# Eight gate sums moved from GpSimd to VectorE, and one accumulator bank taken from another pool

## The chip, the cores and the metric

The kernel runs on one core of a Trainium2 chip. The time is that of one execution on the device, in microseconds. A core has five engines that matter here: TensorE (PE, with its weight loads as PEld), VectorE (DVE), ScalarE (ACT), GpSimd (POOL) and SyncE (SP), which issues most of the DMAs. GpSimd also issues some DMAs, those that add to what they find in memory. Each engine takes its instructions strictly in order.

## What is computed

One decoder layer on 512 tokens of width 1024, all in float32. Three branches are computed from the normalised input u, each an attention and a projection, and each is weighted by a gate:

```python
g = jax.nn.sigmoid(gl.reshape(B, S, N_BRANCH, D))
merged = (g[:, :, 0] * jnp.einsum('bse,ed->bsd', y_swa, w_branch_swa[l])
          + g[:, :, 1] * jnp.einsum('bse,ed->bsd', y_sb, w_branch_sb[l])
          + g[:, :, 2] * jnp.einsum('bse,ed->bsd', y_mem, w_branch_mem[l]))
mix = jnp.einsum('bsd,de->bse', merged, w_out[l])
h = h + rms_norm(mix, ln_mix_post[l])
```

The branches are attention over a band of 128 tokens (swa), stick-breaking attention (sb) and cross-attention to 256 memory vectors (mem, four heads of width 128). A gated feed-forward network of width 2816 follows.

## The kernel before

**Products.** Everything is kept transposed, with 128 channels on the partitions and the 512 tokens along the row. A float32 product is made of three: each factor is split into a high part and a low part (`split`, lines 135 and 136: a cast on ScalarE, a subtraction on VectorE), and `mm3` issues high by high, low by high and high by low (lines 169, 171 and 172). So a factor has to be loaded, cast and subtracted before TensorE can use it.

**Order of the work.** The weights of the projections, gates and branches form one list of units (`dn`). Each unit has a load (ahead by four units), a split (ahead by three) and a generator that issues its products. The attention code runs these products in between: `dn.run(us)` issues units for so many estimated microseconds while softmax work goes on elsewhere. The branches come in the order stick-breaking, banded, memory. A scheduler then places the instructions of each engine by its own estimates and by priority, so the order on an engine isn't the order of the code; code under `tc.high_priority()` goes ahead.

**Joining the branches** (`branch`, from line 578). For each of eight channel blocks c, twelve products give a branch product in an accumulator bank `br`. VectorE multiplies it by the gate (line 592, into the gate's tile `g`). For the stick-breaking branch that tile becomes the accumulator. For the banded branch (`order == 1`) GpSimd adds the tile to the accumulator (line 598). For the memory branch VectorE adds it (line 600), and the result is split for the output projection. The banded branch's eight products are run while the four memory heads go through their softmax (`mem_pair`): scores `ms`, a maximum (line 957) and its negation (line 960), exponentials on ScalarE, a reciprocal (line 965), scalings `mw` on VectorE (line 968), transposes `mpt` on TensorE (line 974), their splits `mpts` (lines 135 and 136), value products `ym` and their splits `y2`.

**The memory gates** are computed as a product of 2x2 blocks with seven instead of eight block products (`quarter`, `add_quarters`), named p1, p2, p5, p6, p3, p7, p4 and taken in this order, twice (n = 0 and 1). Three accumulator banks hold them: x for p1, p6, p7 and p4 on top of each other, w for p2, y for p5 and p3. Each block product is 24 products of 256 columns. In the trace these banks are qx, qw and qy. Behind p1, p5 and p6 ScalarE copies the bank (line 415, `qkp`); behind p2, p3 and p7 VectorE joins the bank and an earlier copy (line 409; for p2 the result is `qj`). The factor of p5 is a sum that a DMA of GpSimd makes (line 377); VectorE then adds p1's weights to it for p6 and p2's for p3 (line 393).

**Accumulator banks.** TensorE has eight banks. Two make up the pool `psd` (`dps`), which takes the units' products: projections, branch products and, before the change, all three banks of the gates. Six make up `psa` (`aps`), which takes the attention's tiles and later the output projection and the feed-forward network. A new tile takes a bank that its last user has given up.

Of the kernel before, what the change touches and what calls it, by code (L numbers as in the profile page):

```python
# [14 lines left out]
ALU = mybir.AluOpType  # L15
# [11 lines left out]
SWA, SB, MEM = 0, 1, 2  # L27
# [76 lines left out]
def tile_kernel(ctx, tc, a):  # L104
    nc = tc.nc
# [12 lines left out]
    def ck(name, dt=F32):  # L118
        return ckp.tile([P, 512], dt, tag="ck", name=name)
# [4 lines left out]
    def dps(name):  # L124
        return psd.tile([P, 512], F32, tag="d", name=name)
# [6 lines left out]
    def split(raw, hi, lo, sign=1.0):  # L132

        if sign == 1.0:
            ins = nc.scalar.copy(hi, raw)  # L135
            lows = nc.vector.tensor_tensor(lo, raw, hi.bitcast(F32), op=ALU.subtract)  # L136
        else:
            ins = nc.scalar.mul(hi, raw, sign)
            lows = nc.vector.scalar_tensor_tensor(lo, raw, sign, hi.bitcast(F32), op0=ALU.mult, op1=ALU.subtract)
        if "behind" in st:  # L140
            after(ins, st["behind"][0])
            after(lows, st["behind"][1])
        return ins
# [23 lines left out]
    def mm3(out, l, r, start, stop, right_last=False):  # L167
        (lh, ll), (rh, rl) = l, r
        one = nc.tensor.matmul(out, lh, rh, start=start, stop=False, skip_group_check=True)  # L169
        two, three = ((ll, rh), (lh, rl)) if right_last else ((lh, rl), (ll, rh))  # L170
        nc.tensor.matmul(out, *two, start=False, stop=False, skip_group_check=True)  # L171
        return one, nc.tensor.matmul(out, *three, start=False, stop=stop, skip_group_check=True)  # L172
# [4 lines left out]
    def cols(hl, o, n):  # L177
        return hl[0][:, o : o + n], hl[1][:, o : o + n]
# [175 lines left out]
    TILE = dict(p1="x", p6="x", p7="x", p4="x", p5="y", p3="y", p2="w")  # L354
    SEVEN = ("p1", "p2", "p5", "p6", "p3", "p7", "p4")
    qw, qb_, qk = {}, {}, {}

    def right_of(p, k):
        if p in ("p1", "p2"):
            return tuple(x[:, :256] for x in u[k if p == "p1" else 4 + k])  # L360
        if p in ("p5", "p3"):
            return tuple(x[:, 256:] for x in u[k if p == "p5" else 4 + k])
        return cols(right[p][k // 2], (k % 2) * 256, 256)
# [33 lines left out]
    def q_end(b, n, p, ps):  # L397
        def done(i, f, src, sign=1.0):
            if b in st.get("sigmoid", ()):
                gate_out(b, n, i, f, src, sign)  # L400
                return
            if sign != 1.0:
                t = ck(f"qr{b}{n}")
                nc.scalar.mul(t[:, :], src[:, :], sign)
                src = t
            st.setdefault(("raw", b), []).append((n, i, f, src))

        def join(t, x, y, op, i, f):
            nc.vector.tensor_tensor(t[:, :], x[:, :], y[:, :], op=op)
            done(i, f, t)  # L410

        with tc.high_priority():
            if p in ("p1", "p5", "p6"):
                qk[p] = ck(f"qk{p}{b}{n}")
                nc.scalar.copy(qk[p][:, :], ps[:, :])
            elif p == "p3":
                t = qk.pop("p6")
                join(t, t, ps, ALU.subtract, 1, 0)
            elif p == "p7":
                t = qk.pop("p5")  # L420
                join(t, t, ps, ALU.subtract, 1, 1)
            elif p == "p2":
                t = ck(f"qj{b}{n}")
                join(t, ps, qk.pop("p1"), ALU.add, 0, 0)
            else:
                done(0, 1, ps, -1.0)

    def quarter(b, n, p):
        def gen(hi, lo):
            if p in ("p1", "p5", "p2"):  # L430
                qb_[TILE[p]] = dps(f"q{TILE[p]}{b}{n}")
            ps = qb_[TILE[p]]
            for j in range(2):
                for k in range(4):
                    first = p in ("p1", "p5", "p2") and j == 0 and k == 0
                    mm3(
                        ps[:, j * 256 : (j + 1) * 256], cols((hi, lo), (j * 4 + k) * P, P), right_of(p, k), first, k == 3
                    )
                    yield 0.36
            q_end(b, n, p, ps)  # L440

        return gen
# [139 lines left out]
    def branch(b, c2, order):  # L582
        def gen(hi, lo):
            for i in range(2):
                c = 2 * c2 + i
                g = st[(f"g{b}", c)] if (f"g{b}", c) in st else quart[(b, c)]
                ps = dps(f"br{b}{c}")
                for k in range(4):
                    mm3(ps[:, :], cols((hi, lo), (i * 4 + k) * P, P), y[(b, k)], k == 0, k == 3)
                    yield 0.65  # L590
                with tc.high_priority():
                    nc.vector.tensor_tensor(g[:, :], ps[:, :], g[:, :], op=ALU.mult)
                if order == 0:
                    st[("acc", c)] = g
                    continue
                acc = st[("acc", c)]
                if order == 1:
                    nc.gpsimd.tensor_tensor(acc[:, :], acc[:, :], g[:, :], op=ALU.add)
                    continue
                nc.vector.tensor_tensor(acc[:, :], acc[:, :], g[:, :], op=ALU.add)  # L600
                h, l = ck(f"mgh{c}", F32R), ck(f"mgl{c}", F32R)
                split(acc[:, :], h[:, :], l[:, :])
                merged[c] = (h, l)

        return gen
# [4 lines left out]
    for h in range(2):  # L610
        for q in range(3):
            n = 3 if q < 2 else 2
# [677 lines left out]
    bank = {}  # L1290
# [316 lines left out]
```

## Time and profile before

| | us |
|---|---|
| median of three runs | 812.18 |
| lowest and highest of them | 811.28, 813.80 |
| the profiled execution, its own time | 813.66 |
| its span, first to last instruction | 811.9 |
| TensorE busy | 798.1 |
| VectorE busy | 619.0 |
| ScalarE busy | 476.7 |
| GpSimd busy | 91.6 |
| mean granted clock of TensorE | 0.995 |

The profile is one execution. A row of its timeline has the start, the duration, the engine, the line in the code, the operation with what it writes and reads, how many such instructions in a row it stands for, and in brackets how long the engine was idle before it and for whom it waited. In a row of a source line stand the shortest, median and longest duration in nanoseconds. Matmuls are pipelined: one that is listed with 0.39 us lets the next start after about 0.23, so the distance from start to start tells the cost, not the listed duration. The granted clock is a share of full speed.

### The profile page before, as it was taken

What the parts mean: (1) busy time and instruction counts of PE and PEld (TensorE: products, weight loads), DVE (VectorE), ACT (ScalarE), POOL (GpSimd) and SP (SyncE); (2) the same over time, 40 slices, a digit from 0 to 9 for tenths busy, and PEclk for the clock granted to TensorE, in tenths of its full rate; (3) what the DMA queues carried; (4) which work ended last, traced back from release to release, by engine and by line L of the source; (5) the groups of instructions that cost most, each with busy time, mean ns of one, the idle gap of its engine ahead of it and who ended that gap; (6) DMA issues with size and microseconds to landing.
All of it is one profiled execution on the core that took longest, in us unless ns stands there. A gap on an engine that the chain in (4) does not pass through costs nothing.

```text
span 811.9 us, 12928 instructions
## 1 busy us (share of the span) xinstructions
PE 798.1 (98%) x4939; PEld 709.7 (87%) x4939; DVE 619.0 (76%) x975; ACT 476.7 (59%) x861; POOL 91.6 (11%) x109
## 2 busy tenths in 40 slices
PE   9999999999999999899999999999999999999996
PEld 6899788778788889689988899999999999988885
DVE  6898678545478887696694869977676777898797
ACT  7466686665766555555572566655555555666673
POOL 1102110000000000331004100100000000205200
PEclk9999999999999999999999999999999999999998
DMA  9343445212241406505568935987777662759902
GB/s 306 128 147 104 141 157 165 70 52 71 61 104 62 120 3 183 128 27 130 156 226 293 252 60 136 265 210 202 189 178 190 179 171 86 177 132 222 209 2 103
DMA packets 41726, 117.68 MB, mean 145 GB/s; under 512 B 4768, under 2 KB 6320, under 8 KB 41664
## 3 DMA queue, kind: packets, MB, share of 16 engines
q1 hardware_dynamic: 31584, 87.77, 33.8%
q0 software_dynamic: 9648, 28.82, 18.9%
q8 instruction: 38, 0.62, 0.3%
q10 hardware_dynamic: 432, 0.27, 0.1%
q14 instruction: 24, 0.20, 0.1%
HBM read 113.18 MB, written 3.67 MB: 144 GB/s over the span
## 4 chain that ended last, share of the span: by engine, by line
PE 50%; DVE 2%; issue 1%; ACT 1%; DVEq 0%
PE gx L172 5%; PE gx L169 5%; PE gx L171 5%; PE x L172 2%; PE x L171 2%; PE x L169 2%; PE gy L169 2%; PE gy L172 2%; PE gy L171 2%; PE mx L172 2%; PE mx L169 2%; PE mx L171 2%; PE y L172 1%; PE y L171 1%; PE y L169 1%; PE gw L172 1%
## 5 line engine op out<-in xcount | busy, mean ns | idle before, releaser
L135 ACT CAST hi<-gw 128x1024 fp32r<-128x1024 f32 x77 | 79.8, 1047 | 81.4 <-DVE gw L1192 39.8
L136 DVE TENSOR_TENSOR lo<-gw,hi 128x1024 fp32r<-128x1024 f32 x77 | 93.6, 1223 | 34.0 <-ACT hi L135 33.9
L135 ACT CAST hi<-raw 128x1024 fp32r<-128x1024 f32 (+2 forms) x52 | 53.1, 1032 | 49.3 <-PE qb L171 11.3
L136 DVE TENSOR_TENSOR lo<-raw,hi 128x1024 fp32r<-128x1024 f32 (+2 forms) x52 | 63.1, 1217 | 18.7 <-ACT hi L135 18.5
L1174 POOL DMA_DIRECT2D gw<-in_w_gu x27 | 23.3, 895 | 190.4 <-DMA gw<-in_w_gu 117.7
L135 ACT CAST hi<-r 128x1024 fp32r<-128x1024 f32 (+1 forms) x24 | 23.6, 981 | 19.9 <-PE y L172 5.3
L171 PE MATMUL x<-lo,lh 128*128 128x512 f32 x88 | 34.3, 390 | 0.0
L169 PE MATMUL x<-hi,lh 128*128 128x512 f32 x88 | 34.3, 389 | 0.0
L172 PE MATMUL x<-hi,ll 128*128 128x512 f32 x88 | 34.1, 389 | 0.0
L136 DVE TENSOR_TENSOR lo<-qw,hi 128x1024 fp32r<-128x1024 f32 x18 | 22.8, 1264 | 11.2 <-ACT hi L135 11.2
L136 DVE TENSOR_TENSOR lo<-r,hi 128x1024 fp32r<-128x1024 f32 (+1 forms) x24 | 27.2, 1132 | 3.9 <-ACT hi L135 3.7
L135 ACT CAST hi<-qw 128x1024 fp32r<-128x1024 f32 x18 | 18.9, 1050 | 16.2 <-issue 6.0
L188 ACT ACTIVATE e<-e 128x384 f32<-128x384 f32 (+1 forms) x48 | 26.9, 561 | 1.5
L834 DVE SCALAR_TENSOR_TENSOR e<-z,e 128x384 f32<-128x384 f32 (+1 forms) x24 | 14.3, 598 | 17.6 <-ACT e L188 17.6
L135 ACT CAST hi<-bp 128x512 fp32r<-128x512 f32 x33 | 19.3, 620 | 13.5 <-PE y L172 4.8
L136 DVE TENSOR_TENSOR lo<-bp,hi 128x512 fp32r<-128x512 f32 x33 | 22.2, 708 | 5.7 <-ACT hi L135 5.5
L172 PE MATMUL gx<-N2h,lo 128*128 128x256 f32 x88 | 25.0, 285 | 0.3 <-DVE lo L136 0.3
L169 PE MATMUL gx<-B11h,hi 128*128 128x256 f32 x88 | 25.1, 285 | 0.2 <-ACT B11h L1103 0.2
L169 PE MATMUL mx<-woh,mgh 128*128 128x512 f32 x64 | 25.0, 391 | 0.0
L172 PE MATMUL gw<-B21h,lo 128*128 128x256 f32 x88 | 25.0, 284 | 0.0
L171 PE MATMUL gx<-B11l,hi 128*128 128x256 f32 x88 | 25.0, 284 | 0.0
L172 PE MATMUL mx<-woh,mgl 128*128 128x512 f32 x64 | 24.9, 390 | 0.0
(920 smaller groups left out, 2986.4 us busy)
## 6 DMA issues: line engine op xcount, KB each, us to landing
gw<-in_w_gu SPq DMA_DIRECT2D x57, 512.0 KB, 5.1
gw<-in_w_gu POOLq DMA_DIRECT2D x27, 512.0 KB, 6.9
raw<-in_w_p SPq DMA_DIRECT2D x26, 512.0 KB, 4.1
qw<-in_w_p SPq DMA_DIRECT2D x15, 512.0 KB, 4.0
raw<-in_w_br SPq DMA_DIRECT2D x12, 512.0 KB, 3.9
bp<-in_w_dn SPq DMA_DIRECT2D x22, 256.0 KB, 8.7
r<-in_w_dn POOLq DMA_DIRECT2D x10, 512.0 KB, 8.1
raw<-in_w_out SPq DMA_DIRECT2D x8, 512.0 KB, 4.5
```

Source lines behind the costliest of these rows:

```text
L135: ins = nc.scalar.copy(hi, raw)
L136: lows = nc.vector.tensor_tensor(lo, raw, hi.bitcast(F32), op=ALU.subtract)
L169: one = nc.tensor.matmul(out, lh, rh, start=start, stop=False, skip_group_check=True)
L171: nc.tensor.matmul(out, *two, start=False, stop=False, skip_group_check=True)
L172: return one, nc.tensor.matmul(out, *three, start=False, stop=stop, skip_group_check=True)
L188: ins = nc.scalar.activation(*args, **kw)
L834: nc.vector.scalar_tensor_tensor(x, z[i][:, :n], 0.0, x, op0=ALU.max, op1=ALU.add)
L1174: nc.gpsimd.dma_start(gw[(n, key)][:, :], g_src(n, i, j), accum_op=ALU.add)
```

## The change

Two edits. The sums that add the banded branch to the accumulator are issued on VectorE instead of GpSimd. In the memory gates the bank y, which p5 opens and p3 uses after it, comes from the pool of six (`aps`) instead of the pool of two (`dps`); the banded branch's gates keep theirs.

```diff
     def quarter(b, n, p):
         def gen(hi, lo):
             if p in ("p1", "p5", "p2"):
-                qb_[TILE[p]] = dps(f"q{TILE[p]}{b}{n}")
+                bank = aps if b == MEM and p == "p5" else dps
+                qb_[TILE[p]] = bank(f"q{TILE[p]}{b}{n}")
...
                 if order == 1:
-                    nc.gpsimd.tensor_tensor(acc[:, :], acc[:, :], g[:, :], op=ALU.add)
+                    nc.vector.tensor_tensor(acc[:, :], acc[:, :], g[:, :], op=ALU.add)
                     continue
```

The scheduler places other instructions differently in consequence. From line 432 on, the changed kernel's lines have numbers higher by one.

On VectorE, at the start of the banded branch, before: the gate products (line 592, on the branch products br), the first head's reciprocal and scalings, and the second head's.

```order
L592 TENSOR_TENSOR g_2970<-br_3403,g_2970 128x512
L957 TENSOR_REDUCE mnm_3366<-ms_3334 128x2
L957 TENSOR_REDUCE mnm_3366<-ms_3335 128x2
L960 TENSOR_SCALAR mnm_3366<-mnm_3366 128x4
L965 RECIPROCAL mden_3351<-mden_3351 128x4
L968 TENSOR_SCALAR mw_3348<-mw_3348,mden_3351 128x256 x2
L592 TENSOR_TENSOR g_3307<-br_3424,g_3307 128x512
L968 TENSOR_SCALAR mw_3349<-mw_3349,mden_3351 128x256 x2
L136 TENSOR_TENSOR lo_3421<-qw_3382,hi_3420 128x1024
```

The same place on VectorE in the changed kernel; line 599 is the moved sum:

```order
L599 TENSOR_TENSOR g_1761<-g_1761,g_2891 128x512
L593 TENSOR_TENSOR g_2970<-br_3403,g_2970 128x512
L958 TENSOR_REDUCE mnm_3366<-ms_3334 128x2
L958 TENSOR_REDUCE mnm_3366<-ms_3335 128x2
L599 TENSOR_TENSOR g_1810<-g_1810,g_2970 128x512
L966 RECIPROCAL mden_3351<-mden_3351 128x4
L961 TENSOR_SCALAR mnm_3366<-mnm_3366 128x4
L593 TENSOR_TENSOR g_3307<-br_3424,g_3307 128x512
L969 TENSOR_SCALAR mw_3348<-mw_3348,mden_3351 128x256 x2
L969 TENSOR_SCALAR mw_3349<-mw_3349,mden_3351 128x256 x2
L136 TENSOR_TENSOR lo_3421<-qw_3382,hi_3420 128x1024
```

Two sums stand among the others, and all four scalings of the first head now come behind the gate product g_3307.

On TensorE, at the first head's transposes, before: the transposes of the first scaled half, three products of the fourth channel block, then the transposes of the second half.

```order
L974 MATMUL mpt_3434<-c_ident,mw_3348 128x128
L974 MATMUL mpt_3435<-c_ident,mw_3348 128x128
L171 MATMUL br_3475<-y00l,hi_3240 128x512
L172 MATMUL br_3475<-y00h,lo_3241 128x512
L169 MATMUL br_3475<-y01h,hi_3240 128x512
L974 MATMUL mpt_3434<-c_ident,mw_3349 128x128
L974 MATMUL mpt_3435<-c_ident,mw_3349 128x128
```

The same place on TensorE in the changed kernel, up to the first transposes:

```order
L171 MATMUL br_3475<-y00l,hi_3240 128x512
L172 MATMUL br_3475<-y00h,lo_3241 128x512
L169 MATMUL br_3475<-y01h,hi_3240 128x512
L171 MATMUL br_3475<-y01l,hi_3240 128x512
L172 MATMUL br_3475<-y01h,lo_3241 128x512
L975 MATMUL mpt_3434<-c_ident,mw_3348 128x128
L975 MATMUL mpt_3435<-c_ident,mw_3348 128x128
```

Six products of br_3475 now stand in front of the transposes, where one stood before, and the transposes of both halves follow in one piece.

On TensorE, in the memory gates with n = 0, before: p2 has ended, nine products of p6 (qx) have begun, and p5 (qy) comes behind them; these are the last four of the nine and the first of p5.

```order
L172 MATMUL qx_3775<-p6rh_2919,lo_3772 128x256
L169 MATMUL qx_3775<-p6rh_2990,hi_3771 128x256
L171 MATMUL qx_3775<-p6rl_2991,hi_3771 128x256
L172 MATMUL qx_3775<-p6rh_2990,lo_3772 128x256
L169 MATMUL qy_3845<-n0h,hi_3607 128x256
L171 MATMUL qy_3845<-n0l,hi_3607 128x256
L172 MATMUL qy_3845<-n0h,lo_3608 128x256
```

The same place on TensorE in the changed kernel, from the last products of p2 (qw) on:

```order
L169 MATMUL qw_3807<-n7h,hi_3573 128x256
L171 MATMUL qw_3807<-n7l,hi_3573 128x256
L172 MATMUL qw_3807<-n7h,lo_3574 128x256
L169 MATMUL qy_3845<-n0h,hi_3607 128x256
L171 MATMUL qy_3845<-n0l,hi_3607 128x256
L172 MATMUL qy_3845<-n0h,lo_3608 128x256
L169 MATMUL qy_3845<-n1h,hi_3607 128x256
```

p5 follows p2 directly, and p6's 24 products stand in one piece behind p5. With n = 1 the same happens, where fourteen products of p6 stood in front of p5.

## The prediction

> **What bounds the kernel now.** I read the page first, then TensorE's own list of waits, then windows around the place where those waits lie, then the timeline of that place. The page says that TensorE works nearly all the time:
>
> ```profile
> span 811.9 us, 12928 instructions
> PE 798.1 (98%) x4939; PEld 709.7 (87%) x4939; DVE 619.0 (76%) x975; ACT 476.7 (59%) x861; POOL 91.6 (11%) x109
> ```
>
> So time can only come out of TensorE's 13.8 us of idleness, or out of stretches in which it works slowly. Its waits on other engines are few (total, times, longest, in us):
>
> ```profile
> PE mpt L974 <- DVE mw L968: 3.0, 1, 3.0
> PE qy L169 <- DVE qj L409: 0.8, 1, 0.8
> PE qy L169 <- ACT qkp L415: 0.4, 1, 0.4
> ```
>
> All three lie in the part of the program that the change touches: the first in the banded branch, where the memory attention's weights are transposed (mpt), the other two in the memory gates' products (qy). The windows, with busy time and count of TensorE, weight loads, VectorE, ScalarE and GpSimd, then granted clock, DMA share and GB/s:
>
> ```profile
> 334.87:350.42 15.55, 12.36 (x65) 10.04 (x64) 14.14 (x21) 6.78 (x16) 5.00 (x4) 0.89 0.21 35
> 350.42:366.00 15.58, 15.58 (x78) 12.89 (x77) 14.14 (x26) 9.22 (x25) 5.04 (x3) 1.00 0.12 34
> 339.60:343.00 3.40, 3.21 (x10) 2.73 (x11) 3.37 (x10) 1.07 (x2) 0.00 (x0) 0.50 0.40 72
> 343.00:344.00 1.00, 1.00 (x11) 0.91 (x9) 0.59 (x1) 0.00 (x0) 0.00 (x0) 1.00 0.00 0
> 430.00:460.00 30.00, 30.00 (x134) 24.86 (x133) 17.99 (x36) 12.11 (x30) 12.58 (x11) 1.00 0.98 294
> ```
>
> The first half of the banded stage lasts as long as the second with fewer products in it, and the granted clock in it is 0.50 from 339.6 to 343 and 1.00 again behind that. The timeline tells why:
>
> ```profile
> 335.87 1.19 POOL L377 DMA_DIRECT2D qw<-in_w_p  x1 [4.15 <-ACT hi L135]
> 336.06 3.93 DVE L968 TENSOR_SCALAR mw<-mw,mden 128x256 f32<-128x256 f32 x2
> 336.34 0.40 PE L169 MATMUL br<-y01h,hi 128*128 128x512 f32 x1
> 336.65 2.92 POOL L598 TENSOR_TENSOR g<-g,g 128x512 f32<-128x512 f32 x2
> 339.79 1.12 PE L974 MATMUL mpt<-c_ident,mw 128*128 128x128 f32 x4 [3.05 <-DVE mw L968]
> ```
>
> Two small scalings on VectorE take 3.93 us and end when GpSimd's DMA issue and its two sums (L598) have ended; TensorE's next transposes wait for them. That this is GpSimd's doing shows in the groups by shape (busy, then mean ns):
>
> ```profile
> L968 DVE TENSOR_SCALAR mw<-mw,mden 128x256 f32<-128x256 f32 x16 | 9.1, 621 | 0.1
> L919 DVE TENSOR_SCALAR w<-w,den 128x256 f32<-128x256 f32 x32 | 9.2, 349 | 0.2
> L393 DVE TENSOR_TENSOR qw<-qw,qw 128x1024 f32<-128x1024 f32 x6 | 9.3, 1545 | 0.1
> L1192 DVE TENSOR_TENSOR gw<-gw,gw 128x1024 f32<-128x1024 f32 x20 | 24.4, 1219 | 0.0
> L600 DVE TENSOR_TENSOR g<-g,g 128x512 f32<-128x512 f32 x8 | 5.5, 685 | 0.0
> L598 POOL TENSOR_TENSOR g<-g,g x8: 1282/1502/2457, 330.4 to 367.6; 128x512 f32<-128x512 f32 x8
> ```
>
> The scaling that runs among the sums has a mean of 621 ns, the same shape elsewhere 349. The weight addition L393 has 1545 against 1219 for its twin. The sums themselves reach 2457 ns. The Trainium skill's page "SBUF — State Buffer", section "Who interferes with whom", says that VectorE and GpSimd share one pair of memory ports as an exclusive lock, for scalings and for sums with two SBUF inputs alike. The trace agrees: the scaling was held until 339.7.
>
> **The change, part 1: the eight sums go to VectorE.** What the stage loses today follows from what its instructions cost where nothing holds them:
>
> ```profile
> 350.06 0.28 PE L169 MATMUL ms<-mks1h,qms3h 128*128 128x256 f32 x1
> 350.18 0.28 PE L171 MATMUL ms<-mks1l,qms3h 128*128 128x256 f32 x1
> 350.42 0.40 PE L169 MATMUL br<-y00h,hi 128*128 128x512 f32 x1
> 353.17 0.39 PE L169 MATMUL br<-y00h,hi 128*128 128x512 f32 x1
> 357.93 1.91 PE L974 MATMUL mpt<-c_ident,mw 128*128 128x128 f32 x16
> 359.60 0.48 PE L169 MATMUL br<-y03h,hi 128*128 128x512 f32 x1
> ```
>
> A score product (ms) follows the one before it after 0.12 us. Twelve 512-column products lie between 350.42 and 353.17, so each is 0.229. Sixteen transposes take 359.60 - 357.93 = 1.67. By the code, the first half (334.87 to 350.42) holds 12 branch and 12 value products, 24 score products and 16 transposes: 24 x 0.229 + 24 x 0.12 + 1.67 = 10.05 us. It takes 15.55, so 5.5 are lost: 3.05 of idleness, 1.6 by the clock (half of the 3.21 us in which TensorE worked at 0.50), the rest in small waits. The second half holds 60 such products and 16 transposes, 15.41 us, and takes 15.58.
>
> What the stage will lose after the change I replay along VectorE's new order, with these rows:
>
> ```profile
> 332.35 0.69 DVE L592 TENSOR_TENSOR g<-br,g 128x512 f32<-128x512 f32 x1 [2.00 <-PE br L172]
> 332.96 1.28 DVE L957 TENSOR_REDUCE mnm<-ms 128x2 f32<-128x512 f32 x2
> 334.64 0.39 PE L172 MATMUL br<-y03h,lo 128*128 128x512 f32 x1
> 341.25 1.14 DVE L968 TENSOR_SCALAR mw<-mw,mden 128x256 f32<-128x256 f32 x4
> ```
>
> Instructions of that size start 0.61 apart (332.35 to 332.96), and a scaling follows another after (1.14 - 0.35) / 3 = 0.26. The two reductions let go at 334.24. The new sum of g_1810 takes 0.6, to 334.84, and reciprocal and negation 0.4, to 335.24. The product on br_3424, ready at 335.03, comes next, to 335.84. Then come the four scalings at 335.84, 336.11, 336.37 and 336.64. TensorE meanwhile has six products of br_3475 in front of the transposes, now moved ahead of them: 334.87 + 6 x 0.229 = 336.24. The first scaling is done at 336.19, the last at 336.99, so the eight transposes end at 337.2, with a wait of 0.15. The next head's transposes, and the first value products that need mpts00l, come out 0.25 late in the same way. In the second half the transposes of head 3 stand behind the product g_3313, which waits for its branch product; there I find 0.25 more. This gives 0.65 us of new waits, none near 3 us, so no clock loss.
>
> What the replay leaves open is GpSimd's DMA issue at 335.87, which stays and falls on the first scaling. The row before shows the scaling held from 336.06, 0.59 us before the sums began, though it needs 0.35; so the DMA issue may hold it too. Its bounds are 0 (the scaling is first, at 335.84) and 1.2 (a whole issue). The nearest row is this same one; which of the two comes first is open within 0.03 us, so I take 0.5. The stage then loses 0.65 + 0.5 = 1.15 instead of 5.5 + 0.17 = 5.67: a gain of **4.5 us**.
>
> VectorE's load covers this. It is busy 28.28 of 31.13 us in the stage; the eight sums add 8 x 0.685 = 5.5, and the stretching that ends gives back 16 x (621 - 349) + 6 x (1545 - 1219) ns = 6.3. Behind the sums on VectorE's queue stand the scalings that the transposes need; that delay is in the replay. GpSimd keeps its weight DMAs, and the sums no longer stand between them; the last waited for a split on VectorE and not for a sum, so nothing is won there:
>
> ```profile
> 375.11 1.20 POOL L377 DMA_DIRECT2D qw<-in_w_p  x1 [5.41 <-DVE lo L136]
> 358.15 1.22 DVE L136 TENSOR_TENSOR lo<-qw,hi 128x1024 fp32r<-128x1024 f32 x1
> ```
>
> The Trainium skill's page "TensorE: Matmul & The Clock Gate", section "What's actually happening", says the clock halves after about 3.4 us of idleness, in a free-running window. Here 3.05 us were enough in the profiled run; by the page it depends on where the window falls, so a timed run may lack the 1.6 us. By that the gain would be 6.2 - 1.6 = 4.6 in such a run.
>
> **Part 2: the bank of p5.** With two banks, qx holds one and qw the other, so qy had to wait until the join qj had emptied qw:
>
> ```profile
> 372.72 0.28 PE L172 MATMUL qx<-p6rh,lo 128*128 128x256 f32 x1
> 373.79 0.39 PE L169 MATMUL qy<-n0h,hi 128*128 128x256 f32 x1 [0.79 <-DVE qj L409]
> 394.61 0.28 PE L171 MATMUL qx<-p6rl,hi 128*128 128x256 f32 x1
> 395.00 0.39 PE L169 MATMUL qy<-n0h,hi 128*128 128x256 f32 x1
> 399.06 0.28 PE L172 MATMUL qx<-p6rh,lo 128*128 128x256 f32 x1
> 399.69 0.39 PE L169 MATMUL qy<-n4h,hi 128*128 128x256 f32 x1 [0.35 <-ACT qkp L415]
> ```
>
> Against a step of 0.12 these three cost 0.95 + 0.27 + 0.51 = 1.73. With a bank of the six, p5 follows p2 at once; its factor was split at 358.15 (the second row above), 15 us before its use. p6 then runs in one piece behind it, so its factor is due later, and p5's copy has 24 products (2.9 us) of cover before p3 needs the bank. I take all of it: **1.7 us**, bounds 0 and 1.7. The six banks' other users, the memory heads, have been emptied by then.
>
> **Sum.** 4.5 + 1.7 = 6.2 us. From 405 on TensorE runs without a hole until the mix (30.00 of 30.00 in the last window above), so what is won early should arrive at the end. The profiled execution took 813.66 (span 811.9 and 1.76 around it), so 813.66 - 6.2 = **807.5 us**. The median of the three runs shown is 812.18, 1.5 lower, about the size of the clock loss; 812.18 - 4.6 gives 807.6, so I leave the forecast there.
>
> **Rivals.** About 0.3%, 2.4 us, is what a measurement of this kernel can tell from no change.
> - *Small waits at every transpose.* GpSimd's DMA issue holds the scalings for a full 1.2 us, each of the four groups of transposes waits 0.6, and 1.0 of the bank's 1.7 is won: 5.67 - 3.6 + 1.0 = 3.1, so 810.6 from the profiled run and 809.1 from the median; I put it at 809.7. For it: VectorE stays 90% busy in order. Against it: the replay's margins.
> - *The gain is absorbed later, or timed runs lack the hole.* From 430 to 460 the DMA share is 0.98; if those loads don't start earlier, the feed-forward's first weights come late by what was won: 812. Against it: TensorE has no hole there, and buffers that the moving work empties release the loads.
> - *VectorE becomes the bound, slower.* If the long rows are VectorE's own and stay, it has 28.28 + 5.5 = 33.8 us of work in a stage of 31.13. That adds 2.7, and two more holes of 3 us cost 1.6 of clock each; less 1.7 for the bank, 813.66 + 4.2 = 817.9. It decides where a scaling stays over 1 us with no sum beside it. Against it: 32 scalings of that shape at 349 ns.
> - *The change doesn't do what it says* would mean that p5 still waits; then 1.7 is missing and the time is 809.2, inside the first rival.
>
> **How the numbers follow.** Forecast 0.62; first rival with the last 0.16; absorbed 0.15; slower 0.07. The low end is the full 7.2 us (no new wait but 0.2) off the median, 805.0; the high end, 810.8, takes in the first rival and the upper edge of the forecast, and leaves the other two out. Faster by over 2.4 us is the forecast and most of the first rival, 0.76; within it 0.17; slower 0.07.
>
> **What would show it.** Right: L968 back near 350 ns each, L393 near 1220, no TensorE wait on mw above 1 us, the granted clock at 1.00 through the stage, no idle row before qy, and the stage shorter by 4 to 5 us. The DMA issue would show as one L968 of up to 1.5 us. Wrong: a TensorE wait of 2 us or more on mw or mpts, a clock window of 0.50, or a new wait on a weight load behind 430.

## The result, and the profile after

The changed kernel takes 806.76 us (median of 4 runs, 806.60 to 806.88), the kernel before 812.73 beside it (4 runs, 811.28 to 813.80): a ratio of 0.9928, with a 95% interval of 0.991 to 0.9945. Run again later (e11 below) it took 806.74 against 813.76, a ratio of 0.9919 (0.9905 to 0.9932). The profiled execution took 806.6 us, 1.8 of it around the span. Two of the 41 runs of the kernel before that were timed beside the experiments took 1595.41 and 4496.57 us, and no number here counts them.

The page of the changed kernel, span and busy time by engine:

```profile
span 804.8 us, 12915 instructions
PE 795.6 (99%) x4939; PEld 708.2 (88%) x4939; DVE 616.2 (77%) x983; ACT 477.0 (59%) x861; POOL 78.9 (10%) x101
```

TensorE has as many instructions as before and 2.5 us less busy time; 4.6 us of its idleness have gone as well. VectorE has taken on eight sums and is 2.8 us less busy than before. TensorE's list of waits begins so (total, times, longest):

```profile
PE warm L175 <- DVE idle L683: 1.4, 1, 1.4
PE gx L172 <- DVE lo L136: 0.3, 1, 0.3
PE kb L169 <- ACT uh L245: 0.2, 1, 0.2
```

All three lie outside the part that was changed, and the list of the kernel before had them too, with 1.3, 0.3 and 0.4 us; the three rows that the prediction shows were not all of it. The waits at mpt and qy are gone. The scalings are now L969, their transposes L975, the sums L599. The stretch of the stage in which the long wait and the slow clock lay, in four windows, and then longer ones, with the columns as in the prediction:

```profile
335.00:338.00 3.00, 3.00 (x18) 2.45 (x17) 2.90 (x8) 3.00 (x11) 1.19 (x1) 1.00 0.00 1
338.00:339.60 1.60, 1.60 (x9) 1.17 (x9) 1.60 (x5) 1.46 (x3) 0.00 (x0) 1.00 1.04 125
339.60:341.50 1.90, 1.90 (x13) 1.61 (x12) 1.90 (x6) 0.76 (x3) 0.00 (x0) 1.00 0.93 169
341.50:343.00 1.50, 1.50 (x10) 1.32 (x9) 1.50 (x4) 1.06 (x3) 0.00 (x0) 1.00 0.05 12
...
334.97:360.95 25.98, 25.98 (x142) 21.71 (x140) 24.86 (x52) 16.80 (x41) 1.19 (x1) 1.00 0.20 41
360.95:398.44 37.49, 37.49 (x313) 37.46 (x312) 24.47 (x24) 20.18 (x31) 1.20 (x1) 1.00 0.54 155
422.90:452.90 30.00, 30.00 (x134) 24.85 (x133) 18.40 (x36) 12.11 (x30) 12.23 (x11) 1.00 0.97 294
398.44:804.80 406.36, 399.04 (x2656) 368.61 (x2654) 321.87 (x481) 227.44 (x396) 52.34 (x56) 1.00 0.67 174
```

TensorE is busy in all of the first four, and their granted clock is 1.00. The fifth row is the whole banded stage, 25.98 us where it was 31.13. The sixth is the memory gates' products. For those, and for all that follows, the windows of the kernel before, cut at the same two instructions:

```profile
366.00:405.54 39.54, 38.29 (x313) 37.65 (x312) 24.85 (x23) 20.56 (x32) 3.33 (x2) 1.00 0.54 146
405.54:811.90 406.36, 399.02 (x2656) 368.65 (x2654) 321.69 (x481) 227.40 (x396) 52.69 (x56) 0.99 0.67 174
```

So the gates are 2.05 us shorter, the stage 5.15, and the remainder takes 406.36 us both times: what was won arrives at the end whole. The seventh row above is the mix, the window that the prediction shows at 430 to 460, seven microseconds earlier and without a hole.

VectorE's groups by shape (busy, then mean ns), after:

```profile
L920 DVE TENSOR_SCALAR w<-w,den 128x256 f32<-128x256 f32 x32 | 9.2, 348 | 0.2
L393 DVE TENSOR_TENSOR qw<-qw,qw 128x1024 f32<-128x1024 f32 x6 | 7.3, 1222 | 0.1
L599 DVE TENSOR_TENSOR g<-g,g 128x512 f32<-128x512 f32 x8 | 5.4, 678 | 0.0
L969 DVE TENSOR_SCALAR mw<-mw,mden 128x256 f32<-128x256 f32 x16 | 4.8, 350 | 0.0
```

The scalings have fallen from 621 ns to the 350 of their twin, L393 from 1545 to 1222. That gives back 4.3 and 2.0 us of VectorE, more than the 5.4 that the sums cost there.

The timeline of the changed kernel, GpSimd's DMA issue, the scalings beside it and the transposes behind them:

```profile
336.17 1.19 POOL L377 DMA_DIRECT2D qw<-in_w_p  x1 [8.11 <-DVE mw L969]
335.78 1.25 DVE L969 TENSOR_SCALAR mw<-mw,mden 128x256 f32<-128x256 f32 x4
336.34 1.18 PE L975 MATMUL mpt<-c_ident,mw 128*128 128x128 f32 x8
```

Eight transposes now run in a row at 336.34 without a wait; in the kernel before, the second four of them came at 339.79.

### The profile page after: what moved, and what is told of

Read it like the earlier page. It is cut to its first block, busy times and chain, and to the rows that moved or that the text cites. A ratio compares the mean times of both kernels' runs of the same rounds, so it can differ in the third digit from the quotient of the medians.

```text
span 804.8 us, 12915 instructions
## 1 busy us (share of the span) xinstructions
PE 795.6 (99%) x4939; PEld 708.2 (88%) x4939; DVE 616.2 (77%) x983; ACT 477.0 (59%) x861; POOL 78.9 (10%) x101
## 4 chain that ended last, share of the span: by engine, by line
PE 95%; DVE 2%; ACT 1%; issue 1%; DMA 1%; DVEq 0%; ACTq 0%
PE gx L172 5%; PE gx L169 5%; PE gx L171 5%; PE z L175 4%; PE g L169 3%; PE br L169 3%; PE br L171 3%; PE g L171 3%; PE g L172 3%; PE br L172 3%; PE x L172 2%; PE x L171 2%; PE x L169 2%; PE gy L171 2%; PE gy L169 2%; PE gy L172 2%
```

## The experiments

The theory is the prediction's: GpSimd's sums hold VectorE's scalings, TensorE stands behind the scalings, and the sums themselves find room on VectorE; p5's bank is worth its three waits, apart from that. The rivals: GpSimd's DMA issue is the holder; the gain comes from the order of VectorE's queue and not from GpSimd being idle; VectorE pays for the sums; the halves depend on each other. The kernel before ran beside each set, with medians of 813.36 (14 runs, e1 to e4), 813.60 (16 runs, e5 to e8) and 813.76 (9 runs, e9 to e11).

**e1: the first half alone.**

```diff
@@ the kernel before, branch()
-                    nc.gpsimd.tensor_tensor(acc[:, :], acc[:, :], g[:, :], op=ALU.add)
+                    nc.vector.tensor_tensor(acc[:, :], acc[:, :], g[:, :], op=ALU.add)
```

> The first half of the change alone: the eight sums run on VectorE, the bank of p5 stays in the pool of two. Theory (GpSimd's sums hold VectorE's scalings, and TensorE waits for those): TensorE's wait at the mpt transposes goes as in the whole change, about 5.1 us of the profiled span, and 1.7 to 2.0 us stay behind with the waits at qy; the median is 1.7 to 2.0 us above that of the whole change, near 808.6. Rival (the halves need each other: with the bank unchanged the gain is given back at qy): 811 or more.

Measured: 808.68 us, ratio 0.9943 (0.993 to 0.9956). Stage and gates of its profiled run:

```profile
334.99:361.15 26.16, 26.15 (x141) 21.72 (x140) 25.08 (x52) 16.85 (x41) 1.19 (x1) 1.00 0.19 41
361.15:400.39 39.24, 38.30 (x314) 37.66 (x312) 24.49 (x24) 19.96 (x31) 1.20 (x1) 1.00 0.52 148
```

The stage is nearly as short as in the whole change (25.98), and the gates are nearly as long as before (39.54). The first half stands by itself.

**e2: the second half alone.**

```diff
@@ the kernel before, quarter()
-                qb_[TILE[p]] = dps(f"q{TILE[p]}{b}{n}")
+                bank = aps if b == MEM and p == "p5" else dps
+                qb_[TILE[p]] = bank(f"q{TILE[p]}{b}{n}")
```

> The second half alone: p5's bank comes from the six, the sums stay on GpSimd. Theory: the two waits at qy go and nothing else, 1.7 to 2.0 us less than before, near 810.8; the 3.0 us wait at mpt stays, and L968 with it near 3.9 us for two. Rival (a wait moved to the next quarter, p3 or p7, takes their place): within 0.5 us of before, near 812.5.

Measured: 811.57 us, ratio 0.9979 (0.9969 to 0.9989). The same windows:

```profile
334.95:365.93 30.98, 28.07 (x142) 22.93 (x140) 28.01 (x46) 16.02 (x40) 10.04 (x7) 0.94 0.17 35
365.93:403.43 37.50, 37.50 (x314) 37.47 (x312) 24.86 (x23) 20.66 (x32) 3.33 (x2) 1.00 0.55 154
```

Here the gates are at 37.50, as in the whole change, and the stage is at 30.98, with its clock loss. The halves add up to within about half a microsecond: by the medians 1.79 us for this one (813.36 - 811.57) and 4.68 for e1 (813.36 - 808.68), 6.47 together, against 7.02 for both in e11 (813.76 - 806.74).

**e3: no sums at all.** The eight sums are left out, so the banded branch is missing from the output.

```diff
@@ the kernel before, branch()
                 if order == 1:
-                    nc.gpsimd.tensor_tensor(acc[:, :], acc[:, :], g[:, :], op=ALU.add)
                     continue
```

> The kernel before with the eight sums left out altogether, so the banded branch is missing from the output; bank and all else as before. Theory (the sums on GpSimd are what holds the scalings; on VectorE they cost next to nothing): the same time as with the sums on VectorE alone, within 0.5 us, near 808.5, L968 near 350 ns. Rival 1 (GpSimd's DMA issue at L377 is what holds them): the wait at mpt stays at 2 us or more, and the time near 811. Rival 2 (the sums on VectorE have a price of their own): shorter than with the sums on VectorE alone by 1 us or more.

Measured: 808.18 us, ratio 0.9939 (0.9926 to 0.9952). That is 0.5 below e1, so 5.4 us of sums on VectorE cost 0.5 of the time. GpSimd's DMA issue is still there, beside two of the scalings. The group of all scalings, and then the timeline:

```profile
L967 DVE TENSOR_SCALAR mw<-mw,mden 128x256 f32<-128x256 f32 x16 | 4.9, 358 | 0.1
```

```profile
336.15 1.19 POOL L377 DMA_DIRECT2D qw<-in_w_p  x1 [7.09 <-DVE mw L967]
336.26 0.75 DVE L967 TENSOR_SCALAR mw<-mw,mden 128x256 f32<-128x256 f32 x2
```

Two scalings beside the issue take 0.75 us, where two in the open take 0.62 (335.13 in this run). With a mean of 358 ns and no wait at mpt, the issue is not the holder. The kernel before shows the other side, a sum with no issue near it:

```profile
354.14 1.29 POOL L598 TENSOR_TENSOR g<-g,g 128x512 f32<-128x512 f32 x1 [7.33 <-DVE mden L965]
354.18 2.19 DVE L968 TENSOR_SCALAR mw<-mw,mden 128x256 f32<-128x256 f32 x4
```

Four scalings take 2.19 us there instead of 1.14; the first of them alone took 1.40. So a sum holds a scaling by itself. No transpose waited at that place, and so it cost nothing.

**e4: idle sums on GpSimd.** The changed kernel, with GpSimd kept as busy as it was, on data that nobody reads.

```diff
@@ the changed kernel, branch()
                     nc.vector.tensor_tensor(acc[:, :], acc[:, :], g[:, :], op=ALU.add)
+                    for e in range(2):
+                        x = g[:, e * 256 : (e + 1) * 256]
+                        nc.gpsimd.tensor_tensor(dump[:, :], x, x, op=ALU.add)
```

> The changed kernel, with the sums on VectorE, and beside each of them two idle sums on GpSimd that read the same product and write a scratch tile that nobody reads: GpSimd is as busy at the same place as before, but no one waits for it. Theory (hold of VectorE by GpSimd's work as such): scalings of over 1 us at L969 and a wait at mpt of 2 us or more come back, 3 to 5 us more than the changed kernel, 810 to 812. Rival (the gain came from the order of VectorE's queue or from the data that no longer pass over GpSimd): within 0.5 us of the changed kernel, near 807, L969 near 350 ns.

Measured: 810.28 us, ratio 0.9963 (0.995 to 0.9976): 3.5 of the change's gain are gone again, with VectorE's and TensorE's work as in the change. The groups, the stage, and TensorE's wait:

```profile
L973 DVE TENSOR_SCALAR mw<-mw,mden 128x256 f32<-128x256 f32 x16 | 7.7, 528 | 0.0
```

```profile
334.90:364.25 29.35, 27.43 (x142) 21.50 (x141) 28.41 (x52) 16.82 (x41) 11.66 (x13) 1.00 0.18 37
```

```profile
PE mpt L979 <- DVE mw L973: 1.7, 6, 0.7
```

The hold is back and so is the wait, though in another shape than expected: no scaling is over 0.77 us and the wait comes in six pieces, since each idle sum is half as long as a real one (0.61 us at its shortest, against 1.28). The stage is 3.37 longer than the change's, with 1.92 of idleness. The other 1.45 are busy time (27.43 against 25.98): TensorE runs many of the transposes one pair at a time between the pieces, and the pairs no longer overlap. In the group of all transposes, e4 first, then the changed kernel:

```profile
L979 PE MATMUL mpt<-c_ident,mw 128*128 128x128 f32 x32 | 5.8, 287 | 1.9 <-DVE mw L973 1.7
```

```profile
L975 PE MATMUL mpt<-c_ident,mw 128*128 128x128 f32 x32 | 4.5, 275 | 0.0
```

So 1.3 of the 1.45 are the transposes' own. The list of waits shows only half of what a wait in pieces costs.

**e5: the scalings on ScalarE.** The sums stay on GpSimd.

```diff
@@ the kernel before, mem_pair()
-                nc.vector.tensor_scalar(x, x, den[:, n : n + 1], None, op0=ALU.mult)
+                nc.scalar.mul(x, x, den[:, n : n + 1])
```

> The kernel before, with the scalings of L968 on ScalarE instead of VectorE; the eight sums stay on GpSimd and the bank as it was. Theory (the sums hold VectorE's scalings, and those alone reach TensorE): the single wait of 3 us at mpt goes, ScalarE's scalings stay near their own length beside a GpSimd sum, and the time falls to that of the sums on VectorE alone or a little above it, 808.5 to 809.7. Rival 1 (the softmax chain is late by itself, whoever scales): 812 or more. Rival 2 (ScalarE is held as well): scalings of over 1 us on ScalarE, 811 or more.

Measured: 808.56 us, ratio 0.9948 (0.9935 to 0.9962), the same time as e1 within 0.2. GpSimd's sums and ScalarE's scalings in its timeline:

```profile
336.98 4.23 POOL L598 TENSOR_TENSOR g<-g,g 128x512 f32<-128x512 f32 x3
340.33 1.74 ACT L968 ACTIVATE mw<-mw,mden 128x256 f32<-128x256 f32 x4
354.52 1.73 ACT L968 ACTIVATE mw<-mw,mden 128x256 f32<-128x256 f32 x4
```

Four scalings take 1.74 us partly beside a sum, and 1.73 with none beside them: ScalarE isn't held. Both sides of the hold can be moved away, with one result.

**e6: the scalings in another form.** They also sum their result into a scratch column; the sums stay on GpSimd.

```diff
@@ the kernel before, mem_pair()
-                nc.vector.tensor_scalar(x, x, den[:, n : n + 1], None, op0=ALU.mult)
+                nc.vector.tensor_scalar(
+                    x, x, den[:, n : n + 1], None, op0=ALU.mult, op1=ALU.add, accum_out=junk[:, n : n + 1]
+                )
```

> The kernel before, with the scalings of L968 in the form that also sums its result into a scratch column; sums on GpSimd, bank as it was. The Trainium skill (SBUF — State Buffer, Who interferes with whom) has this form outside the two-port modes, and free of GpSimd. If so: each scaling is longer by itself, about 410 ns by half of the 512-column sum's rate (678 ns) plus its fixed part, and the read of the sum behind it, but none is over 1 us beside a GpSimd sum; the wait of 3 us at mpt goes, 808.7 plus 0 to 1.5 for the longer scalings. Rival (any VectorE instruction waits while GpSimd works on the memory): scalings of over 1 us, the wait at mpt stays over 2 us, 812.5 or more.

Measured: 813.15 us, ratio 1.0004 (0.9994 to 1.0014). The expectation held for the instruction and failed for the time. The scalings of all heads (shortest, median, longest ns), and then what stood beside GpSimd's sums in the timeline:

```profile
L968 DVE TENSOR_SCALAR_CACHE_REDUCE mw<-mw,mden x16: 461/473/482, 335.0 to 363.9; 128x256 f32<-128x256 f32 x16
```

```profile
336.47 2.98 POOL L598 TENSOR_TENSOR g<-g,g 128x512 f32<-128x512 f32 x2
336.77 0.48 DVE L968 TENSOR_SCALAR_CACHE_REDUCE mw<-mw,mden 128x256 f32<-128x256 f32 x1
338.37 2.17 DVE L136 TENSOR_TENSOR lo<-qw,hi 128x1024 fp32r<-128x1024 f32 x1
345.06 1.55 PE L976 MATMUL mpt<-c_ident,mw 128*128 128x128 f32 x8 [0.70 <-DVE mw L968]
363.29 1.55 PE L976 MATMUL mpt<-c_ident,mw 128*128 128x128 f32 x8 [0.84 <-DVE mw L968]
```

A scaling at 336.77, in the middle of two sums that run from 336.47 to 339.45, took its 0.48 us. So not every VectorE instruction is held; the split at 338.37, with two memory operands, still was, 2.17 us instead of 1.21. By the Trainium skill's page "SBUF — State Buffer", section "Who interferes with whom", the form with an accumulator stays off the shared ports, and these rows agree. But a scaling now follows the one before it after 0.40 us (336.38 and 336.77 in that timeline) instead of 0.26. TensorE waits for the first scaling of a block, 0.70 and 0.84 us in the last two rows, and then takes the transposes at the scalings' pace: a block of eight lasts 1.55 us, where one in the kernel before lasted 1.03:

```profile
343.14 1.03 PE L974 MATMUL mpt<-c_ident,mw 128*128 128x128 f32 x8
```

Idle time of 1.8 and that slower pace for four groups of eight, about 2, are nearly the 4.0 us by which the span of e6's profiled run is longer than e1's (810.7 and 806.7), where the hold is gone without a new price.

**e7: the sums twice on VectorE.** The changed kernel with the loop of e4, its sums on VectorE.

```diff
@@ e4
-                        nc.gpsimd.tensor_tensor(dump[:, :], x, x, op=ALU.add)
+                        nc.vector.tensor_tensor(dump[:, :], x, x, op=ALU.add)
```

> The changed kernel with VectorE's added work about doubled: beside each of the eight sums two half sums of the same product into a scratch tile that nobody reads, some 16 times 0.41 us, 6.6 us. Theory (VectorE has slack in this stage, its queue does not bound): 0 to 1.5 us more than the changed kernel, 806.8 to 808.3, waits at mpt in pieces below 0.5 us. Rival (VectorE is near its bound there, 24.9 busy of 26.0 us, and what is added shows in full): 4 to 6 us more, 811 or above.

Measured: 807.44 us, ratio 0.9932 (0.9919 to 0.9945), 0.7 above the change. TensorE's list of waits has none on mw or mpt. So VectorE is not the bound.

**e8: GpSimd only writes.**

```diff
@@ the changed kernel, branch()
                     nc.vector.tensor_tensor(acc[:, :], acc[:, :], g[:, :], op=ALU.add)
+                    for _ in range(3):
+                        nc.gpsimd.memset(g[:, :], 0.0)
```

> The changed kernel with GpSimd writing only: behind each sum, three fills of the product's dead tile with zeros, which read nothing. By the Trainium skill (SBUF — State Buffer, Who interferes with whom) a scaling in a two-port mode is held by any GpSimd work, a sum of two memory operands only by such as reads. If so: scalings at L969 beside a fill are held (over 500 ns), VectorE's sums at L393 and L599 are not (1220 and 678 ns), and the time is 0.5 to 3 us above the changed kernel's. Rival (only reads hold): L969 near 350 ns throughout and 807.

Measured: 808.44 us, ratio 0.9945 (0.9931 to 0.996), 1.7 above the change. Its groups:

```profile
L393 DVE TENSOR_TENSOR qw<-qw,qw 128x1024 f32<-128x1024 f32 x6 | 7.3, 1223 | 0.1
L971 DVE TENSOR_SCALAR mw<-mw,mden 128x256 f32<-128x256 f32 x16 | 7.3, 504 | 0.0
L599 DVE TENSOR_TENSOR g<-g,g 128x512 f32<-128x512 f32 x8 | 5.4, 678 | 0.0
```

The scalings are held by fills: 504 ns in the mean, 1102 at most, and that longest one had part of a DMA issue beside it as well. What has two memory operands is not held. Of VectorE's instructions of that kind, the sums of L599 show little, since they hardly stood beside a fill; a weight addition of L393 did:

```profile
355.15 1.70 POOL L601 MEMSET g<- 128x512 f32 x3 [1.12 <-DVE g L599]
356.26 1.22 DVE L393 TENSOR_TENSOR qw<-qw,qw 128x1024 f32<-128x1024 f32 x1
```

It took the 1.22 us that it takes in the open, and so did the split before it (1.21 from 355.01 on), which stood beside fills for nearly all of its time. The section of the Trainium skill's page "SBUF — State Buffer" named at e6 makes this very difference between GpSimd work that reads and work that only writes.

**e9, e10 and e11: the other way round, both, and the change again.** e9 is the kernel before with e2's bank and e5's scalings on ScalarE. e10 is the changed kernel with e5's scalings. e11 is the changed kernel again. Their expectations follow in the order e11, e9, e10.

> The changed kernel once more, beside the next two on one chip: 806.6 to 806.9, and none of its times above 808, since no stall of TensorE over 1.5 us is left in it.

> The other way round the hold: the sums stay on GpSimd, the scalings of L968 go to ScalarE, and p5's bank comes from the six as in the change. Theory (both ways only take the scaling out of GpSimd's reach, and the bank is worth 1.7 to 2.0 either way): 808.56, measured for the scalings on ScalarE with the bank unchanged, less 1.5 to 2.0, so 806.6 to 807.1, the same as the changed kernel within 0.3. Rival (ScalarE, with 5.7 us more of scalings, is late with the copies behind qy): 807.8 or more.

> The whole change, and the scalings of L968 on ScalarE too. Theory (nothing is left to win, TensorE waits for no one for over 0.3 us in this stage of the changed kernel): within 0.5 us of the changed kernel, 806.3 to 807.3. Rival (the scalings' pace on VectorE still holds the transposes): 806 or less.

Measured: e11 806.74 (806.51 to 806.86), as expected. e9 807.50, ratio 0.9929 (0.9916 to 0.9943): 0.8 above e11, more than the theory gave and less than the rival. Its list of waits has one of 0.4 on a join of the gates (qx on L409), which the changed kernel doesn't have. The transposes also come in eleven blocks instead of five, and a 512-column product next to such a block lets the next instruction start after 0.32 us (337.34 to 337.66) instead of 0.23. That may be the other 0.4; no run tests it by itself. e10 808.59, ratio 0.9947 (0.9933 to 0.996): the theory fell, it is 1.85 slower than the change. Its first wait:

```profile
PE qx L169 <- DVE qkp L409: 1.9, 1, 1.9
```

It stands at 381.50, in the gates, where p4 adds to a bank that a join on VectorE has to read first. In VectorE's queue that join comes behind a split of 1.23 us, and the split behind a conversion on ScalarE. The order had come out differently, and there is a new wait where there was none. The change as it was made is the fastest of the kernels tried here.

## Why the prediction was right

The forecast was 807.5; 806.76 is 0.7 below it, for the reason that was given.

- *The hold.* Right: e4 brings it back with work that no one waits for, e5 and e3 remove it in two other ways. L969, L393, the clock and the waits came out as written under "What would show it"; only the stage is shorter by 5.15, a little more than the 4 to 5 written there. The DMA issue shows as one scaling of 0.46 us.
- *Part 1, 4.5 us.* The profiled stage gave 5.15. Of the 1.15 us that it was to lose after the change, it loses 0.52 (25.98 against 31.13 - 5.67 = 25.46). The DMA issue was mis-sized at 0.5: the scaling came first, at 335.78 against 336.17, and the four took 1.25 us where four in the open take 1.14, so 0.1. In e1 the issue came at 335.94 and the four took 1.46, so 0.3, and no more in e7, where it came first (335.70 against 335.81, the four again 1.46). Only in e8, where it came first by 0.08 us, did the first scaling take 0.79 instead of 0.35, which is the size that the prediction gave it. The waits of the replay, 0.65, are then about 0.4.
- *Part 2, 1.7 us.* From e1 to the change the gates go from 39.24 to 37.49, 1.75. From the kernel before to e2 they lose 2.04. Those 0.3 more are in the step behind the prediction's three rows, which it left out. In the kernel before, each of the three products that came late let the next one start only after 0.22 us instead of 0.12, so three times 0.1. The first of them started at 373.79, and the next is this:

```profile
374.01 0.28 PE L171 MATMUL qy<-n0l,hi 128*128 128x256 f32 x1
```

  The other two pairs start at 395.00 and 395.23, and at 399.69 and 399.91.
- *The sum.* Of the 0.9 us by which the profiled run beats the forecast, 0.63 are in the stage and 0.3 in the gates.
- *The median.* The clock loss was put at 1.6 us, present in some runs. Over the 39 runs of the kernel before in the three sets above, the 24 with a mean granted clock of 0.996 or less took 813.28 to 815.62 (median 813.77), the 8 with 0.998 or more 810.92 to 812.79 (812.13): 1.64 apart. The other 7, at 0.997, lie across both (811.16 to 813.79). The 8 runs of the changed kernel have 0.998 or 0.999 and lie within 0.4 us. So the change also ends this spread. Its gain is 5.4 us against runs without the loss, where 4.6 was forecast, and 7.0 against those with it, where 6.2 was.
- *The rivals.* Small waits at every transpose: TensorE's list has none on mw, though e4 shows that they can cost 3.5. Absorbed later: the remainder is 406.36 both times. VectorE becomes the bound: e7 adds more work yet for 0.7. That the change doesn't do what it says: qy starts at 366.70, 0.12 behind the last qw, so it does.

## What to carry to other kernels

Where two engines work on the memory at once, compare one instruction's mean with its twin elsewhere: a difference of 1.8 times showed that something held it, and the timeline beside it showed what, before anything was moved. Then ask who stands behind the held instruction: here 5.4 us of work on the busier engine cost 0.5 us, because moving it there ended the hold. And cost a wait in pieces at more than its idle time, because what runs between the pieces loses its overlap as well.

## What the runs showed of the hardware

- TensorE's clock fell after idleness of 3.05 us in the kernel before, and after less. In e2, one row each from the list of the waiting transposes and from the windows:

```profile
339.60 0.95 PE L975 MATMUL mpt<-c_ident,mw 128*128 128x128 f32 x4 [2.77 <-DVE mw L969]
```

```profile
340.00:342.00 2.00, 2.00 (x7) 1.67 (x7) 1.97 (x6) 1.07 (x2) 0.00 (x0) 0.50 0.45 81
```

- In e10's profiled run it fell after 1.95 us, and that run took 810.42, the other four 808.46 to 808.90:

```profile
381.50 0.58 PE L169 MATMUL qx<-p4rh,hi 128*128 128x256 f32 x1 [1.95 <-DVE qkp L409]
```

```profile
381.50:386.00 4.50, 4.50 (x25) 4.50 (x26) 2.31 (x2) 0.71 (x2) 0.00 (x0) 0.62 0.23 47
```

The Trainium skill's page "TensorE: Matmul & The Clock Gate", section "What's actually happening", gives about 3.4 us of idleness in a free-running window. The measured holes are shorter, and that the loss comes in some runs and not in others fits the free-running part. What decides in a single run stays open.

- Where GpSimd's instructions came back to back, the hold lasted over both: in e2 two scalings took 3.65 us from 336.15 on, beside two sums that lasted 2.93 from 336.45 on. In e4, with sums half as long, four of them ran from 336.54 to 340.90 and VectorE's scalings got in between: none took over 0.77 us.
